# Weight sums on GpSimd, low parts in three-operand form, and seven-product down projections in four rounds instead of two

## The chip, the core and the metric

The kernel runs on one core of a Trainium2 chip. The metric is the device time of one execution in microseconds. Five engines work side by side and wait for each other through semaphores: TensorE (PE: matmuls into PSUM; PEld: its weight loads), VectorE (DVE), ScalarE (ACT), GpSimd (POOL) and SyncE (SP), which here issues most of the transfers from memory.

## The reference

Two layers of a hybrid decoder trunk on 528 tokens (16 learned meta tokens and 512 inputs) of width 1024, in float32. After the second layer only the 512 real tokens are kept. Each layer is an attention stage (a forgetting-attention group and a retention group of heads, one input and one output projection) and a feed-forward stage (FFN) of width 2816:

```python
def hybrid_layer(h, attn_norm_g, w_in, b_fgate, ret_gn_g, w_out,
                 ffn_norm_g, w_gate, w_up, w_down, cos, sin):
    ...
    mix = jnp.concatenate([fox_out, ret_out], axis=-1)
    h = h + jnp.einsum('blc,cd->bld', mix, w_out)

    hn = rmsnorm(h, ffn_norm_g)
    ff = jax.nn.silu(jnp.einsum('bld,df->blf', hn, w_gate)) * jnp.einsum('bld,df->blf', hn, w_up)
    return h + jnp.einsum('blf,fd->bld', ff, w_down)
```

The change touches the FFN alone. The final RMSNorm after layer 1 is untouched.

## The kernel before

**Layout.** Activations lie transposed: a tile `h[k]` holds 128 of the 1024 features as partitions and the tokens as columns. The 2816 columns of the FFN are 22 tiles of 128, numbered by `f`, 0 to 21.

**Three matmuls for one.** A float32 matmul is made as three matmuls in the format fp32r. Each operand is split into a high part (its rounding to fp32r, a copy on ScalarE) and a low part (the remainder, `src - hi`, a subtraction on VectorE); the products high x high, high x low and low x high are added in PSUM. The helper `split` (L154) does this for activations, `splits` (L940) for weights; the lines that appear in the profile are L155 for the former, L941 (rounding) and L942 (low part) for the latter. In the attention stage `convert` (L177) splits weights, and there the low parts of many weight tiles are made on GpSimd, in pieces of 128 columns (L208).

**Units.** From `f = 2` on (`PLAIN`), gate tile `f` and up tile `f` are computed together by the class `Unit` (L1055). The two output tiles, the two halves of the tokens (264 columns each, in layer 1 256) and the two halves of the 1024 input features form a 2 x 2 x 2 block product, and this is done with seven block products instead of eight. The price is sums of blocks ahead and behind. On the weight side they are, with `a` the gate weights and `b` the up weights in eight blocks of 128 x 128, `HB` = 4 of them a half:

```python
                    nc.vector.tensor_add(s[:, HB:NK], b[:, 0:HB], b[:, HB:NK])
                    nc.vector.tensor_sub(s[:, 0:HB], s[:, HB:NK], a[:, 0:HB])
                    splits(hi, lo, s)
```

(L1084 to L1086 in `make2`), and one more sum in `make3` (L1092) and in `make4` (L1098). So a unit has four sums of 128 x 512 on VectorE and splits of 1024, 1024, 1024 and 512 columns. On the token side the sums are made once a layer by `x_forms` (L905). Behind the products, `keep` (L1112) and `done` (L1127) add the partial results out of PSUM (L1124, L1131), apply the norm, SiLU and the product of gate and up (L1133 to L1139), and split the activation (L1143 to L1148). A layer has 20 units.

**Down projection in rounds.** The FFN width is worked off in `ROUNDS` of two or four tiles `f`. When the activations of a round are ready, their part of the down projection is computed during the units of the next round, one pair of output tiles of `h` beside each unit (four pairs, eight tiles). In a plain round `down` (L1181) makes 48 half-width matmuls for a pair and two additions to `h` (L1202 or L1204). In a round that stands in `SEVENTHS` the class `Pair` (L992) makes the pair in seven block products with 42 half-width matmuls. It needs sums of the down weights (L1012, L1013, L1018, L1020, 256 columns each), splits of 512, 512, 512 and 256 columns (L1011 to L1021), six additions to `h` (L1039, L1041), and sums of the two token halves of the activations, called forms 1 to 4, which `token_forms` (L963) makes when a unit of that round is done (L971, L982, and their splits). Form 1 is made in the first two units of a round, forms 2, 3 and 4 in the last two. Forms 2 and 3 are kept in the second token halves of `st["x"]`, which are no longer read then, form 4 in the tiles `sqh` and `sql`. Rounds 2 and 4 are in `SEVENTHS`; their pairs run beside the units of rounds 3 and 5. The last round is worked off at the end, by itself.

**What sets the order.** Only TensorE's order is written out by hand: the list `steps` in `ffn` (L861) is run in program order. The other engines' instructions are placed by a scheduler according to their dependencies and priorities, and each engine then works its queue in order. Weight tiles are jobs: `need(j)` (L935) converts job `j` and as many of the following as its `reach` says. High and low parts of weights go into two rings of buffers, three deep (`fwhi`, `fwlo`) and two deep (`whi`, `wlo`); a rounding waits until TensorE has read the buffer that it overwrites. Raw gate and down weights share four buffers (`raw`), up weights have two (`fraw`), the sums `S` two.

Of the kernel before, what the change touches and what calls it, by code (L numbers as in the profile page):

```python
# [10 lines left out]
F32 = mybir.dt.float32  # L11
F32R = mybir.dt.float32r
AF = mybir.ActivationFunctionType
ALU = mybir.AluOpType
# [11 lines left out]
NF = DFF // 128  # L26
ROUNDS = ((0, 2), (2, 6), (6, 10), (10, 14), (14, 18), (18, 22))
PLAIN = 2
SEVENTHS = (2, 4)
SEVEN = (0, 1, 2, 3)  # L30
HB = NK // 2
EPS = 1e-6
# [9 lines left out]
def hybrid_kernel(ctx, tc, x_t, w_in, w_fl, w_out, w_gate, w_up, w_down, vecs, b_fg, rope, decay, mask, ident, out_t):  # L42
# [92 lines left out]
    def sv(t, real, p0=0, p1=128):  # L135
        if real:
            return t[p0:p1, META:T]
        return t[p0:p1, 0:T].rearrange("p (a b) -> p a b", a=2)
# [15 lines left out]
    def split(hi, lo, src, pinned=False):  # L154
        return [pin(f, pinned).ins for f in (nc.scalar.copy(hi, src), nc.vector.tensor_sub(lo, src, hi.bitcast(F32)))]  # L155
# [705 lines left out]
    def ffn(l, st, real, last):  # L861
# [29 lines left out]
        def u_done(f):  # L891
            def go(ps):
                u = tt("tq")
                with tc.high_priority() if f == PLAIN - 1 else ExitStack():
                    nc.vector.scalar_tensor_tensor(sv(u, real), pv(ps, real), RSC, sv(st["R"], real), ALU.mult, ALU.mult)
                nc.vector.tensor_mul(sv(u, real), sv(u, real), sv(sgs[f], real))
                fh, fl = act_tile(f)
                split(sv(fh, real), sv(fl, real), sv(u, real))
                acts[f] = (fh, fl)
            return go  # L900

# [3 lines left out]
        def x_forms(k):  # L905
            def go():
                if k == 0:
                    st["t"] = [[fft(f"t{p}{i}", shape=(128, 2, 4, w)) for p in "hl"] for i in range(2)]
                s = fft("S", F32, (128, 6, w), 2)
                a, b = ((h[k][:, c0:c1], h[HB + k][:, c0:c1]) for c0, c1 in HC)  # L910
                g0, g1 = vcol(V_FFN + l * NK + k), vcol(V_FFN + l * NK + HB + k)
                with tc.issue_after(st["scaled"].ins) if real else ExitStack():
                    nc.scalar.activation(s[:, 0:2], two(h[k]), AF.Copy, scale=g0)
                nc.vector.tensor_sub(s[:, 2], s[:, 1], s[:, 0])
                for i in range(2):
                    nc.vector.scalar_tensor_tensor(s[:, 3 + i], b[1], g1, s[:, 1 + i], ALU.mult, ALU.subtract)
                nc.vector.scalar_tensor_tensor(s[:, 5], a[1], g1, s[:, 4], ALU.mult, ALU.subtract)
                th, tl = (t[:, k % 2] for t in st["t"][k // 2])
                split(th, tl, s[:, 2:6])
            return go  # L920

        def t_form(i):
# [16 lines left out]

        def splits(hi, lo, src):  # L940
            nc.scalar.copy(hi, src)  # L941
            nc.vector.tensor_sub(lo, src, hi.bitcast(F32))  # L942

        def product(j, o, x, bank, fresh, final, n=HB, done=None):

# [17 lines left out]
        def token_forms(f, u2):  # L963

            r = seventh(f)[0]
            f0 = ROUNDS[r][0]
            k = (f - f0) % 2
            first = [two(t)[:, 1] for t in acts[f0 + k]]
            if f - f0 < 2:
                halves[k] = u2  # L970
                nc.vector.tensor_sub(u2[:, 0], u2[:, 1], u2[:, 0])  # L971
                split(*first, u2[:, 0])
                forms[r, 1, k] = first
                return
            if k == 0:
                forms[r] = [tt("sqh", F32R), tt("sql", F32R)]
            (a, b), (c, d) = ([t[:, i] for i in range(2)] for t in (halves.pop(k), u2))
            four = [two(t)[:, k] for t in forms[r]]
            second, third = ([two(t)[:, 1] for t in st["x"][i]] for i in (2 + k, k))
            for n, o, x, y, (hi, lo) in ((3, b, d, b, third), (2, d, d, a, second), (4, c, c, d, four)):  # L980
                with tc.high_priority() if k and n < 4 else ExitStack():
                    nc.vector.tensor_sub(o, x, y)  # L982
                    split(hi, lo, o)
                forms[r, n, k] = hi, lo

        def form(r, n):
            return lambda k: forms[r, n, k]
# [67 lines left out]
        class Unit:  # L1055
# [24 lines left out]
            def make2(self, hi, lo):  # L1080
                a, b = self.t["a"], self.t["b"]
                s = self.t["s"] = fft("S", F32, (128, NK, 128), 2)
                with tc.high_priority() if self.f == PLAIN else ExitStack():
                    nc.vector.tensor_add(s[:, HB:NK], b[:, 0:HB], b[:, HB:NK])  # L1084
                    nc.vector.tensor_sub(s[:, 0:HB], s[:, HB:NK], a[:, 0:HB])
                    splits(hi, lo, s)  # L1086


            def make3(self, hi, lo):
                a, b = self.t["a"], self.t["b"]  # L1090
                with tc.high_priority(60) if self.f == PLAIN else ExitStack():
                    nc.vector.tensor_sub(b[:, 0:HB], a[:, 0:HB], b[:, 0:HB])  # L1092
                    splits(hi, lo, b)


            def make4(self, hi, lo):
                a, s = self.t["a"], self.t["s"]
                nc.vector.tensor_sub(a[:, HB:NK], a[:, HB:NK], s[:, 0:HB])  # L1098
                splits(hi, lo, a[:, HB:NK])

            def bank(self, n):
# [25 lines left out]
            def done(self):  # L1127
                e = self.t["e"]
                sg = tt("sg")
                with tc.high_priority():  # L1130
                    nc.vector.tensor_add(two(sg), self.t["zy"][:, :, 0:w], e[:, 0:2])  # L1131
                c = slice(t0, T)
                nc.vector.scalar_tensor_tensor(sg[:, c], sg[:, c], RSC, st["R"][:, c], ALU.mult, ALU.mult)  # L1133
                silu(sg[:, c], None if self.f < NF - 1 else ROOTS if last else LOGS)
                u = tt("tq")
                nc.vector.scalar_tensor_tensor(u[:, c], sg[:, c], RSC, st["R"][:, c], ALU.mult, ALU.mult)
                u2 = two(u)
                nc.vector.tensor_mul(u2[:, 0], self.t["x"][:, 0:w], u2[:, 0])
                nc.vector.tensor_mul(u2[:, 1], e[:, 2], u2[:, 1])  # L1139
                fh, fl = act_tile(self.f)  # L1140
                acts[self.f] = (fh, fl)
                if not seventh(self.f):
                    split(fh[:, c], fl[:, c], u[:, c])  # L1143
                    return
                if self.f - ROUNDS[seventh(self.f)[0]][0] < 2:
                    split(two(fh)[:, 0], two(fl)[:, 0], u2[:, 0])
                else:
                    split(fh[:, c], fl[:, c], u[:, c])  # L1148
                token_forms(self.f, u2)

            def head(self):
# [62 lines left out]
        for r, (f0, f1) in enumerate(ROUNDS):  # L1214
            for f in range(f0, f1):
                if f < PLAIN:
                    if f == 0:
                        st["first"] = range(len(jobs), len(jobs) + 3)
                    steps += dense_steps(w_gate[l, f], [(0, xs, NK, QC, g_done(f) if f else held.append)], banks=f == 1, own=own, far=f == 1, after=st["after"][2 * f])
                    steps += dense_steps(w_up[l, f], [(0, xs, NK, QC, u_done(f))], own=None if f else own, far=f == 0, after=st["after"][1 + 2 * f])  # L1220
                    continue
                for i in (f, f + 1) if f == PLAIN else (f,):
                    if i not in units:
                        units[i] = Unit(i)
                        steps += units[i].head()
                u = units[f]
                p, g0, g1 = fills.pop(0)
                seven = r - 1 in SEVENTHS and p in SEVEN
                after = r - 1 in SEVENTHS and p + 1 in SEVEN or r in SEVENTHS and f == f1 - 1 and 0 in SEVEN
                if seven:  # L1230
                    pair = Pair(r - 1, p)
                    u.rest()
                    pair.rest()
                    u.last()
                    jobs[u.w3]["reach"] = 5 if after else 4
                    d, m, t = pair.steps(), u.middle(), u.tail()
                    steps += d[0] + m[:NK] + d[2] + m[NK:] + d[1] + d[3] + t[:HB] + d[4] + t[HB:] + d[5] + d[6]
                    continue
                u.rest()
                steps += u.middle()  # L1240
                j = down_job(p, g0, g1)
                jobs[j]["reach"] = 4 if after else 3
                steps += down(j, 0, 2 * p, g0, g1, not real or f < PLAIN + 2)
                u.last()
                steps += u.tail()
                steps += down(j, 1, 2 * p + 1, g0, g1, f == PLAIN)
            fills = [(p, f0, f1) for p in range(NK // 2)]
# [379 lines left out]
```

## Time and profile before

| | |
|---|---|
| median of 3 runs | 1249.71 us (1249.49 to 1250.49) |
| span of the profiled execution | 1248.2 us, its granted TensorE clock 0.998 |
| TensorE, VectorE, ScalarE, GpSimd busy | 1236.6, 1062.2, 733.5, 294.6 us |
| FFN units of layer 0 | from about 320 to 609 us of the span |
| FFN units of layer 1 | from about 935 to 1213 us |
| GpSimd busy in these | 0 us |

The span runs from the first to the last instruction of the profiled execution; the runs that were timed lie 1.3 to 2.3 us above it. Busy times are sums of instruction spans without overlap. A line of a group gives the line of the kernel, the engine, the operation, the tile written and the tiles read, the shapes, the count, the total and the mean time, and the idle time of the engine before it. In a table of stages each line is a stretch of the span: its length, then busy time and instruction count of each engine, the granted clock and the share of the DMA engines. In a timeline the first number is the start in us, the second the time that the merged instructions cover.

### The profile page before, as it was taken

Reading aid. Unit: us, or ns where it says so; the run is one execution under the profiler, and the core shown is the slowest. Engines: PE = TensorE matmul, PEld = TensorE weight load, DVE = VectorE, ACT = ScalarE, POOL = GpSimd, SP = SyncE. Lnnn points to the kernel's source line nnn. Section 1 sums busy time; section 2 is a strip of 40 time slices with the busy share of each in tenths; the row PEclk is TensorE's granted clock in tenths of the full one; section 3 lists DMA queues with packets and bytes.
Section 4 is the critical chain, followed back from the end, with each engine's and each line's share of the span. In section 5 each row is a group of like instructions: output and inputs, shape, how many; then the busy total and the mean of one; then the engine's idle time right before and its main releaser. Section 6 shows DMA issues by size and latency. Waiting matters only on the chain.

```text
span 1248.2 us, 24164 instructions
## 1 busy us (share of the span) xinstructions
PE 1236.6 (99%) x9387; PEld 1192.1 (96%) x9387; DVE 1062.2 (85%) x2033; ACT 733.5 (59%) x1397; POOL 294.6 (24%) x568
## 2 busy tenths in 40 slices
PE   9999999999999999999999999999999999999997
PEld 9999999999999999999999989999799999999996
DVE  7887756889997999899876877568999989998996
ACT  7767655776544555455566766567765445454554
POOL 4555655440000000000035556554400000000000
PEclk9999999999999999999999999999999999999999
DMA  6222222222433233322312222231414333333322
GB/s 238 68 77 69 78 69 85 60 85 72 133 119 102 85 102 118 103 86 85 114 65 85 63 84 75 68 94 52 141 54 135 111 102 102 100 104 102 102 69 69
DMA packets 43347, 116.25 MB, mean 93 GB/s; under 512 B 5088, under 2 KB 9952, under 8 KB 43232
## 3 DMA queue, kind: packets, MB, share of 16 engines
q1 hardware_dynamic: 42800, 114.41, 28.8%
q8 instruction: 74, 1.21, 0.4%
q14 instruction: 41, 0.34, 0.1%
q10 hardware_dynamic: 432, 0.29, 0.1%
HBM read 112.58 MB, written 2.10 MB: 92 GB/s over the span
## 4 chain that ended last, share of the span: by engine, by line
PE 90%; DVE 5%; ACT 2%; DMA 1%; issue 1%; SPq 0%; ACTq 0%; DVEq 0%
PE psd L231 28%; PE psa L953 22%; PE psd L953 15%; PE psd L1197 8%; PE psa L231 5%; PE psa L1197 3%; PE psa L452 2%; PE psa L619 2%; PE psa L549 1%; PE psa L753 1%; PE psa L789 1%; DMA raw<-w_down 1%; DVE wlo L942 1%; DVE fwlo L942 0%; PE psa L312 0%
## 5 line engine op out<-in xcount | busy, mean ns | idle before, releaser
L208 POOL TENSOR_TENSOR wlo<-raw,whi 128x128 fp32r<-128x128 f32 x488 | 254.6, 557 | 212.2 <-ACT whi L204 212.2
L231 PE MATMUL psd<-xh,whi 128*128 128x264 f32 (+1 forms) x696 | 169.7, 313 | 0.0
L231 PE MATMUL psd<-xh,wlo 128*128 128x264 f32 (+1 forms) x696 | 161.0, 301 | 0.0
L231 PE MATMUL psd<-xl,whi 128*128 128x264 f32 (+1 forms) x696 | 160.6, 300 | 0.0
L231 PEld LDWEIGHTS psd<-xh,whi 128*128 128x128 f32 x696 | 112.6, 190 | 3.3 <-ACT whi L204 0.3
L231 PEld LDWEIGHTS psd<-xh,wlo 128*128 128x128 f32 x696 | 111.1, 188 | 4.4
L231 PEld LDWEIGHTS psd<-xl,whi 128*128 128x128 f32 x696 | 111.7, 189 | 2.5
L941 ACT CAST fwhi<-raw 128x512 fp32r<-128x512 f32 (+2 forms) x88 | 66.2, 757 | 72.3 <-PE psd L953 28.7
L204 ACT CAST whi<-raw 128x512 fp32r<-128x512 f32 (+1 forms) x140 | 82.1, 612 | 32.5 <-PE psd L231 17.3
L127 POOL MEMSET kc<- 64x528 f32 x4 | 2.1, 534 | 367.5 <-PE psd L1197 367.3
L942 DVE TENSOR_TENSOR fwlo<-raw,fwhi 128x512 fp32r<-128x512 f32 (+2 forms) x88 | 75.1, 854 | 7.5 <-ACT fwhi L941 7.4
L941 ACT CAST whi<-raw 128x1024 fp32r<-128x1024 f32 (+2 forms) x72 | 56.8, 789 | 37.6 <-PE psd L953 21.1
L1117 ACT COPY e<-psa 128x264 f32<-128x264 f32 (+1 forms) x120 | 44.9, 374 | 53.5 <-PE psa L953 51.9
L953 PE MATMUL psa<-th,fwhi 128*128 128x264 f32 (+1 forms) x248 | 70.4, 284 | 0.0
L953 PE MATMUL psa<-tl,fwhi 128*128 128x264 f32 (+1 forms) x248 | 70.1, 283 | 0.0
L953 PE MATMUL psa<-th,fwlo 128*128 128x264 f32 (+1 forms) x248 | 70.1, 283 | 0.0
L953 PE MATMUL psa<-th,whi 128*128 128x264 f32 (+1 forms) x232 | 65.4, 282 | 0.0
L942 DVE TENSOR_TENSOR wlo<-raw,whi 128x1024 fp32r<-128x1024 f32 (+1 forms) x72 | 64.1, 893 | 1.5 <-ACT whi L941 1.4
L953 PE MATMUL psa<-tl,whi 128*128 128x264 f32 (+1 forms) x232 | 65.4, 282 | 0.0
L953 PE MATMUL psa<-th,wlo 128*128 128x264 f32 (+1 forms) x232 | 65.3, 281 | 0.0
L566 ACT ACTIVATE pr<-pr,nmax 128x144 f32<-128x144 f32 (+1 forms) x64 | 36.8, 575 | 45.7 <-DVE nmax L553 26.3
L941 ACT CAST fwhi<-S 128x1024 fp32r<-128x1024 f32 (+1 forms) x34 | 28.8, 846 | 34.0 <-PE psa L953 14.3
(442 smaller groups left out, 4381.7 us busy)
## 6 DMA issues: line engine op xcount, KB each, us to landing
raw<-w_in SPq DMA_DIRECT2D x54, 512.0 KB, 3.5
raw<-w_gate SPq DMA_DIRECT2D x44, 512.0 KB, 3.5
fraw<-w_up SPq DMA_DIRECT2D x40, 512.0 KB, 3.5
raw<-w_down SPq DMA_DIRECT2D x80, 256.0 KB, 3.7
raw<-w_out SPq DMA_DIRECT2D x16, 512.0 KB, 3.5
h<-x_t SPq DMA_DIRECT2D x8, 264.0 KB, 4.5
dec<-decay SPq DMA_DIRECT2D x8, 264.0 KB, 2.7
raw<-w_up SPq DMA_DIRECT2D x4, 512.0 KB, 3.9
```

Of the source, the lines that this page charges most:

```text
L204: pin(nc.scalar.copy(hi, job["raw"][:, c0:c1]), pinned)
L208: pin(sub(lo[:, c:c + step], job["raw"][:, c0 + c:c0 + c + step], hi[:, c:c + step].bitcast(F32)), pinned)
L231: nc.tensor.matmul(ps[1][b][:, 0:c1 - c0], w[:, wk, :], x[:, c0:c1], start=(k == 0 and i == 0), stop=(k == n - 1 and i == 2))
L452: nc.tensor.transpose(ps[:, 128 * j:128 * j + 128], src[:, o:o + 128], idt)
L549: nc.tensor.matmul(sc[0:nq, 0:c1 - c0], qq[:, q0:q0 + nq], kk[:, c0:c1], start=(i == 0), stop=(i == 1))
L566: nc.scalar.activation(pr, pr, AF.Exp, bias=nmax[0:nq], scale=-1.0, accum_out=rsum)
L619: nc.tensor.matmul(po[:, c0:SEQ], v[:, j, :], pp[:, j, META + c0:T], start=(j == 0 and i == 0), stop=(j == 4))
L941: nc.scalar.copy(hi, src)
L942: nc.vector.tensor_sub(lo, src, hi.bitcast(F32))
L953: nc.tensor.matmul(bank()[:, 0:b.shape[-1]], a[:, o + k, :], b, start=(fresh and k == 0 and i == 0), stop=(k == n - 1 and i == 2), skip_gr ...
L1117: nc.scalar.copy(self.t["e"][:, i], self.t["x"][:, 0:w])
L1197: nc.tensor.matmul(v[:, 0:c1 - c0], a[:, s * n + k, :], b[:, c0:c1], start=(k == 0 and i == 0), stop=(k == n - 1 and i == 2))
```

## The change

It has four parts.

1. The four weight sums of a unit go to GpSimd, each as four instructions of 128 x 128 (`aside`).
2. In the FFN the low parts are made with `scalar_tensor_tensor`, `(src * 1.0) - hi`, in place of `tensor_sub`: in `splits` and in `halve`, which replaces `split` there. They stay on VectorE, the roundings on ScalarE.
3. `SEVENTHS` goes from two rounds a layer to four: rounds 1, 2, 3 and 4. The pairs of all rounds but the first (two tiles wide) and the last are then made in seven products.
4. Since a round in `SEVENTHS` can now follow another, the tiles of forms 2, 3 and 4 may still be read by the pairs of the round before. `later_form` makes one form; where the round before is in `SEVENTHS` too, the forms of the third unit and form 4 of both units are made during the last unit of the round, behind the products that last read their tiles. Form 4 is now computed as c - a from the tiles that are there, forms 2 and 3 as before.

```diff
-SEVENTHS = (2, 4)
+SEVENTHS = (1, 2, 3, 4)
...
         def splits(hi, lo, src):
             nc.scalar.copy(hi, src)
-            nc.vector.tensor_sub(lo, src, hi.bitcast(F32))
+            nc.vector.scalar_tensor_tensor(lo, src, 1.0, hi.bitcast(F32), ALU.mult, ALU.subtract)
+
+        def halve(hi, lo, src):
+            return [f.ins for f in (nc.scalar.copy(hi, src), nc.vector.scalar_tensor_tensor(lo, src, 1.0, hi.bitcast(F32), ALU.mult, ALU.subtract))]
+
+        def aside(op, out, p, q):
+            for k in range(out.shape[1]):
+                op(out[:, k], p[:, k], q[:, k])
...
             if f - f0 < 2:
                 halves[k] = u2
                 nc.vector.tensor_sub(u2[:, 0], u2[:, 1], u2[:, 0])
-                split(*first, u2[:, 0])
+                halve(*first, u2[:, 0])
                 forms[r, 1, k] = first
                 return
-            if k == 0:
+            halves[k] = halves[k], u2
+            if r - 1 not in SEVENTHS:
+                for n in (3, 2, 4):
+                    later_form(r, n, k)
+            elif k:
+                for n in (2, 3):
+                    later_form(r, n, k)
+
+        def later_form(r, n, k):
+            (a, b), (c, d) = ([t[:, i] for i in range(2)] for t in halves[k])
+            if n == 4 and k == 0:
                 forms[r] = [tt("sqh", F32R), tt("sql", F32R)]
...
+            o, x, y = {2: (a, d, a), 3: (b, d, b), 4: (c, c, a)}[n]
+            hi, lo = [two(t)[:, k] for t in forms[r]] if n == 4 else [two(t)[:, 1] for t in st["x"][k if n == 3 else 2 + k]]
+            with tc.high_priority() if k and n < 4 else ExitStack():
+                nc.vector.tensor_sub(o, x, y)
+                halve(hi, lo, o)
+            forms[r, n, k] = hi, lo
+
+        def later_forms(r, n, *ks):
+            return [lambda k=k: later_form(r, n, k) for k in ks] if r in SEVENTHS and r - 1 in SEVENTHS else []
...
-                    nc.vector.tensor_add(s[:, HB:NK], b[:, 0:HB], b[:, HB:NK])
-                    nc.vector.tensor_sub(s[:, 0:HB], s[:, HB:NK], a[:, 0:HB])
+                    aside(nc.gpsimd.tensor_add, s[:, HB:NK], b[:, 0:HB], b[:, HB:NK])
+                    aside(nc.gpsimd.tensor_sub, s[:, 0:HB], s[:, HB:NK], a[:, 0:HB])
                     splits(hi, lo, s)
...
-                    nc.vector.tensor_sub(b[:, 0:HB], a[:, 0:HB], b[:, 0:HB])
+                    aside(nc.gpsimd.tensor_sub, b[:, 0:HB], a[:, 0:HB], b[:, 0:HB])
...
-                nc.vector.tensor_sub(a[:, HB:NK], a[:, HB:NK], s[:, 0:HB])
+                aside(nc.gpsimd.tensor_sub, a[:, HB:NK], a[:, HB:NK], s[:, 0:HB])
...
-                    steps += d[0] + m[:NK] + d[2] + m[NK:] + d[1] + d[3] + t[:HB] + d[4] + t[HB:] + d[5] + d[6]
+                    i = r if f == f1 - 1 else None
+                    steps += (d[0] + m[:NK] + d[2] + m[NK:] + d[1] + later_forms(i, 2, 0) + d[3] + t[:HB] + d[4]
+                              + later_forms(i, 3, 0) + t[HB:] + d[5] + d[6] + later_forms(i, 4, 0, 1))
```

More of the change, by code (lines that the diff above doesn't have):

```diff
@@ L897, in go @@
                 fh, fl = act_tile(f)
-                split(sv(fh, real), sv(fl, real), sv(u, real))
+                halve(sv(fh, real), sv(fl, real), sv(u, real))
                 acts[f] = (fh, fl)
@@ L918, in go @@
                 th, tl = (t[:, k % 2] for t in st["t"][k // 2])
-                split(th, tl, s[:, 2:6])
+                halve(th, tl, s[:, 2:6])
             return go
@@ L971, in token_forms @@
                 nc.vector.tensor_sub(u2[:, 0], u2[:, 1], u2[:, 0])
-                split(*first, u2[:, 0])
+                halve(*first, u2[:, 0])
                 forms[r, 1, k] = first
                 return
-            if k == 0:
-                forms[r] = [tt("sqh", F32R), tt("sql", F32R)]
[L977 to L984, printed above, removed]
+            halves[k] = halves[k], u2
[8 more added lines that the diff above has]
+            if n == 4 and k == 0:
+                forms[r] = [tt("sqh", F32R), tt("sql", F32R)]
+            o, x, y = {2: (a, d, a), 3: (b, d, b), 4: (c, c, a)}[n]
[6 more added lines that the diff above has]
+            return [lambda k=k: later_form(r, n, k) for k in ks] if r in SEVENTHS and r - 1 in SEVENTHS else []
         def form(r, n):
@@ L1142, in done @@
                 if not seventh(self.f):
-                    split(fh[:, c], fl[:, c], u[:, c])
+                    halve(fh[:, c], fl[:, c], u[:, c])
                     return
                 if self.f - ROUNDS[seventh(self.f)[0]][0] < 2:
-                    split(two(fh)[:, 0], two(fl)[:, 0], u2[:, 0])
+                    halve(two(fh)[:, 0], two(fl)[:, 0], u2[:, 0])
                 else:
-                    split(fh[:, c], fl[:, c], u[:, c])
+                    halve(fh[:, c], fl[:, c], u[:, c])
                 token_forms(self.f, u2)
```

## The prediction

> **What bounds the kernel now.** I read the page first (engine shares, slices, chain), then the busy times of the engines by stage, the waits of TensorE in the FFN stages, the groups of VectorE by shape, and two stretches of the timeline in which GpSimd and VectorE work side by side.
>
> ```profile
> span 1248.2 us, 24164 instructions
> PE 1236.6 (99%) x9387; PEld 1192.1 (96%) x9387; DVE 1062.2 (85%) x2033; ACT 733.5 (59%) x1397; POOL 294.6 (24%) x568
> ...
> DVE  7887756889997999899876877568999989998996
> ...
> POOL 4555655440000000000035556554400000000000
> ...
> PE 90%; DVE 5%; ACT 2%; DMA 1%; issue 1%; SPq 0%; ACTq 0%; DVEq 0%
> ```
>
> TensorE is the bound: 99% busy, 90% of the chain. GpSimd works only in the two attention stretches; in both FFN stretches, which the change edits, it is idle. There VectorE's slices stand at 8 and 9, so the average of 85% hides a second engine near its limit. The stages show it:
>
> ```profile
> core 0: us, PE busy (x) PEld busy (x) DVE busy (x) ACT busy (x) POOL busy (x), PEclk, DMA share, GB/s
> ...
> 372.00:404.30 32.30, 32.30 (x267) 32.30 (x267) 25.85 (x43) 14.58 (x23) 0.00 (x0) 1.00 0.33 98
> 404.30:436.50 32.20, 32.20 (x267) 32.20 (x266) 32.14 (x61) 16.49 (x31) 0.00 (x0) 1.00 0.28 83
> 436.50:497.90 61.40, 61.40 (x506) 61.40 (x506) 61.03 (x107) 31.80 (x49) 0.00 (x0) 1.00 0.33 105
> ...
> 985.40:1016.30 30.90, 30.90 (x217) 28.86 (x216) 25.73 (x42) 14.36 (x23) 0.00 (x0) 1.00 0.37 116
> ...
> 1047.50:1106.80 59.30, 59.30 (x489) 58.51 (x489) 58.87 (x105) 30.38 (x49) 0.00 (x0) 1.00 0.34 107
> ...
> sum 566.50, PE 566.50 PEld 556.87 DVE 538.12 ACT 286.43 POOL 0.00; mean PE 40.46 PEld 39.78 DVE 38.44 ACT 20.46 POOL 0.00
> ```
>
> The sum is over all stages from the end of unit 2 to the end of unit 21 in both layers. A line is two units with plain down rounds (372 to 404.3, 985.4 on), two units that also make token forms (404.3 on), or four units with seven-product down rounds (436.5 on, 1047.5 on). In the last kind VectorE is busy 61.03 of 61.40 us: it only just keeps up, while ScalarE is at half and the clock is 1.00. TensorE still waits for nobody there:
>
> ```profile
> PE psd L1197 <- DVE al L155: 0.2, 1, 0.2
> PE psd L1197 <- ACT ah L155: 0.2, 1, 0.2
> ```
>
> These are all of TensorE's waits from 320 to 1213 us. So seven products pay in full today, but VectorE has 566.5 - 538.1 = 28 us left in both FFNs, nearly all in plain units.
>
> **What TensorE gains.** A plain pair of output tiles is 2 x 4 x 3 x 2 = 48 half-width matmuls, a seven-product pair 7 x 2 x 3 = 42. By the stages a plain unit lasts 32.30/2 = 16.15 us against 61.40/4 = 15.35, in layer 1 30.90/2 = 15.45 against 59.30/4 = 14.83: 0.6 to 0.8, I take 0.70. Rounds 1 and 3 (units 2 to 5 and 10 to 13, whose pairs run in the next round) become seven-product ones: 8 pairs a layer, 16 in all, 11.2 us. If TensorE stays the bound, the FFN stages take 555.3 us and the kernel, counted from the median of 1249.7 (the profiled span is 1.5 us below it), 1238.5.
>
> **What VectorE loses and gains.** Its groups:
>
> ```profile
> L1092 DVE TENSOR_TENSOR fraw<-raw,fraw 128x512 f32<-128x512 f32 x40 | 27.3, 684 | 0.0
> L1085 DVE TENSOR_TENSOR S<-S,raw 128x512 f32<-128x512 f32 x40 | 27.3, 684 | 0.2 <-DMA raw<-w_gate 0.2
> L1098 DVE TENSOR_TENSOR raw<-raw,S 128x512 f32<-128x512 f32 x40 | 27.3, 683 | 0.0
> L1084 DVE TENSOR_TENSOR S<-fraw 128x512 f32<-128x512 f32 x40 | 27.0, 684 | 0.3 <-DMA fraw<-w_up 0.3
> L942 DVE TENSOR_TENSOR wlo<-raw,whi 128x1024 fp32r<-128x1024 f32 x32 | 39.0, 1219 | 1.5 <-ACT whi L941 1.4
> L942 DVE TENSOR_TENSOR fwlo<-raw,fwhi 128x512 fp32r<-128x512 f32 x48 | 32.8, 683 | 0.0
> L1012 DVE TENSOR_TENSOR S<-raw 128x256 f32<-128x256 f32 x16 | 6.7, 419 | 3.1 <-DMA raw<-w_down 3.1
> L1041 DVE TENSOR_TENSOR h<-psa,h 128x264 f32<-128x264 f32 x32 | 13.6, 426 | 0.1
> L1204 DVE TENSOR_TENSOR h<-psd,h 128x528 f32<-128x528 f32 x19 | 13.3, 702 | 0.9 <-PE psd L1197 0.8
> L982 DVE TENSOR_TENSOR tq<-tq 128x264 f32<-128x264 f32 x12 | 5.1, 424 | 0.0
> L1133 DVE SCALAR_TENSOR_TENSOR sg<-sg,R 128x528 f32<-128x528 f32 x20 | 14.0, 700 | 0.0
> L155 DVE TENSOR_TENSOR al<-tq,ah 128x528 fp32r<-128x528 f32 x18 | 12.6, 702 | 0.8 <-ACT ah L155 0.7
> ```
>
> In a queue an instruction costs the distance of starts, not its duration. The stretch that also prices the sharing with GpSimd gives it:
>
> ```profile
> 879.65 0.83 DVE L825 SCALAR_TENSOR_TENSOR d<-d,gn,r 128x512 f32<-128x512 f32 x1
> ...
> 879.88 3.17 POOL L208 TENSOR_TENSOR rql<-raw,rqh 128x128 fp32r<-128x128 f32 x4
> ...
> 880.58 0.77 DVE L818 TENSOR_TENSOR d<-d,sg 128x512 f32<-128x512 f32 x1
> ...
> 882.03 0.69 DVE L155 TENSOR_TENSOR mxl<-d,mxh 128x512 fp32r<-128x512 f32 x1 [0.69 <-ACT mxh L155]
> ...
> 882.64 1.83 DVE L208 TENSOR_TENSOR wlo<-raw,whi 128x512 fp32r<-128x512 f32 x2
> ...
> 883.01 3.53 POOL L208 TENSOR_TENSOR rkl<-raw,rkh 128x128 fp32r<-128x128 f32 x4
> ...
> 884.39 1.82 DVE L208 TENSOR_TENSOR fwlo<-raw,fwhi 128x512 fp32r<-128x512 f32 x2
> ...
> 886.13 0.68 DVE L843 TENSOR_TENSOR h<-psd,h 128x512 f32<-128x512 f32 x1
> ```
>
> The one at 882.03 lasts 0.69 and the next starts 0.61 later: 0.08 of each duration overlaps. So 512 columns cost 0.604, 1024 cost 1.14, 528 cost 0.62, 256 and 264 cost 0.34 and 0.345.
>
> - Sums of gate and up weights leave: 4 x 40 x 0.604 = 96.6 us off.
> - A seven-product pair adds four sums of 256 columns (L1012 and its like), three low parts of 512 and one of 256, five additions of a half (L1041) and a full one: 3 x 0.604 + 5 x 0.338 + 5 x 0.346 + 0.62 = 5.85. It saves one low part of 1024 and two full additions, 1.14 + 1.24 = 2.38. 16 x 3.47 = 55.5 us on.
> - Token forms in two more rounds a layer: in the first two units three instructions of 264 replace one of 528 (+0.41 each), in the other two come six (2.07 each): 4.97 a round, four rounds, 19.9 us on.
> - Low parts in three-operand form: L1133 (three operands, both tensors in SBUF) takes 700 ns for 528 columns, L155 702. Free.
>
> VectorE's own work becomes 538.1 - 96.6 + 55.5 + 19.9 = 516.9 us, below TensorE's 555.3. ScalarE gets more roundings, but it is busy 286 of 566 us. Later forms are made behind the products that last read their tiles and are due a unit later; I cost the order at nothing.
>
> The Trainium skill ("Vector Engine (DVE) Microarchitecture Reference", "Points that are easy to get wrong") says that the three-operand form with two SBUF sources wider than bf16 runs at half throughput. The rows L1133 and L155 contradict it.
>
> **What GpSimd's pieces cost VectorE.** GpSimd gets 16 pieces a unit, 640 in all. What one costs alone, and what both engines do together:
>
> ```profile
> L208 POOL TENSOR_TENSOR wlo<-raw,whi 128x128 fp32r<-128x128 f32 x488 | 254.6, 557 | 212.2 <-ACT whi L204 212.2
> ```
>
> Its own time is no bound: 16 x 0.557 = 8.9 us of a 15 us unit. But from 882.64 to 886.13 four queued VectorE instructions of 512 columns take 3.49 us, 0.87 each and not 0.604, and GpSimd's pieces take 0.88 each: the two engines take turns, and every piece lets VectorE stand 0.27 us. From 879.65 on the delays are (0.83 - 0.69) + (0.77 - 0.69) + 0 + 4 x 0.27 = 1.30 us for eight pieces, 0.16 each. The line with the tile d, gn, r is a three-operand one and waits as well. The bounds of the price are thus 0 (the piece falls beside an instruction that reads PSUM, or beside an idle VectorE) and 0.27.
>
> The Trainium skill ("SBUF — State Buffer", "Who interferes with whom") says that a VectorE instruction with two SBUF inputs and a GpSimd instruction that reads SBUF share a port pair, and that the second to come is blocked for the whole of the first. The trace agrees in kind; in size a piece of 557 ns costs 0.27, not 0.557, and by 0.557 on every piece 640 of them would cost 356 us.
>
> Two prices decide. VectorE has 555.3 - 516.9 = 38.4 us to give, 0.060 us a piece; above that it is the bound. At (566.5 - 516.9)/640 = 0.078 the whole gain is eaten. With a seven-product down pair in its unit VectorE runs nine instructions from PSUM (six additions to h, L1124, L1131, L1138), beside which a waiting piece goes free; with two long ones, some ten of 16. The other six meet a queue without a hole and cost 0.27: 1.62 us a unit, 0.101 a piece, 64.8 us. That is 516.9 + 64.8 = 581.7 against 566.5: +15.2, so **1265 us**. I take this value because it lies between the bounds and because in the units that count VectorE has almost no idle time into which pieces could fall: the six units from 404.3 to 497.9 hold 32.14 + 61.03 = 93.2 us of its work; without their sums (6 x 2.42) and forms (2 x 2.07), and with a seven-product pair in two more of them (2 x 3.47), that is 81.5, or 13.6 a unit, and with the new forms (4.97/4) 14.8 of 15.35 us. From 0.085 to 0.13 a piece the time is 1254 to 1283.
>
> The chain gets longer too: eight pieces before the first mixed rounding, up to 8 x 0.88 = 7 us where VectorE took 1.2. The cover is that roundings wait for weight buffers that TensorE frees, not for sums:
>
> ```profile
> ACT fwhi L941 <- PE psa L953: 40.2, 15, 3.9
> ```
>
> Without that cover each unit would lie up to 5.8 - 3.9 = 2 us later; this is in the upper end of the range.
>
> **Rivals.** *TensorE stays the bound (faster).* The pieces fall into holes, or queued three-operand instructions keep the port pair. For it speaks one stretch:
>
> ```profile
> 26.68 0.84 DVE L428 SCALAR_TENSOR_TENSOR z<-z,R 8x528 f32<-8x528 f32 x1
> 27.45 0.69 DVE L465 SCALAR_TENSOR_TENSOR tq<-tq,R 128x528 f32<-128x528 f32 x1
> 28.07 0.69 DVE L479 SCALAR_TENSOR_TENSOR tq<-tq,R 128x528 f32<-128x528 f32 x1
> ...
> 26.03 3.66 POOL L208 TENSOR_TENSOR wlo<-raw,whi 128x128 fp32r<-128x128 f32 x3
> ```
>
> Behind L428 two three-operand instructions follow at 0.69, undelayed, while three pieces take 3.66 us. The change makes all low parts such instructions. Against it: sums and differences of pairs and forms stay two-operand, and GpSimd needs its 16 turns somewhere. Under 0.060 a piece the time is 1238.5; chance 0.36. Between 0.074 and 0.081 it comes out level, 0.09.
>
> *Every piece pays as in the stretch at 880 us.* 0.16 x 640 = 102.4: 619.3 against 566.5, 1302 us. Against it: that stretch has no PSUM instruction until its end. From 1283 up, 0.11.
>
> *Three-operand low parts take two steps a column.* From 512 to 1024 columns L942 grows by 536 ns; a unit has 3584 + 528 columns of low parts, so 8 x 0.536 = 4.3 us a unit, 172 us over 40, above 1400. L1133 speaks against it: 0.01. This is what the rule of the Trainium skill on that form would do here.
>
> **How the numbers follow.** My forecast has 0.43; slower by more than 0.2% (2.5 us, about what this measurement can tell) is 0.43 + 0.11 + 0.01 = 0.55, level 0.09, faster 0.36. The forecast's own range is 1254 to 1283; to hold the time eight times in ten it reaches down to the first rival, 1237, and up to 1290.
>
> **What would show it.** In the units of rounds 2 to 4 VectorE busy all the time and units longer than 15.35 us; low parts above 1220 and 684 ns; TensorE waiting for weight low parts; GpSimd pieces near 0.9 us. I am wrong if these units still last 15.3 and 14.8 us with VectorE showing idle time: then pieces cost less than 0.060 us.

## The result and the profile after

The changed kernel takes 1324.55 us (median of 4 runs, 1323.62 to 1325.96) against 1249.82 (median of 4): a ratio of 1.0599, 95% interval 1.0583 to 1.0614, slower by 75 us. The direction was forecast, the size was not: 1265 was said, and 1290 as the upper end. All times below are medians of four runs, but for the kernel with the sums left out, where one of the four took 6870.92 us and the median is that of the other three.

The page of the changed kernel, the lines that answer to those of before:

```profile
span 1321.7 us, 25373 instructions
PE 1259.3 (95%) x9483; PEld 1208.6 (91%) x9483; DVE 1120.3 (85%) x2105; ACT 757.6 (57%) x1477; POOL 727.1 (55%) x1208
...
DVE  7877747896999999999867776478969999999996
...
POOL 4555655507757474757055556555195666657540
...
PE 48%; DVE 41%; issue 5%; ACT 3%; POOL 2%; DMA 1%; DVEq 0%; SPq 0%; ACTq 0%; POOLq 0%
```

VectorE's average is the same 85%, and it says nothing: the chain tells that VectorE now holds 41% of the time and TensorE 48%, not 5% and 90%. GpSimd works through both FFNs.

The stages of layer 0 that answer to the first three lines of before's table. The end of a unit is here the start of its addition L1131 (now L1149), and a stretch has the name of the units behind whose ends it lies: units 6 and 7 run from the end of unit 6 to the end of unit 8. So the lines are units 6 and 7, 8 and 9, and 10 to 13:

```profile
core 0: us, PE busy (x) PEld busy (x) DVE busy (x) ACT busy (x) POOL busy (x), PEclk, DMA share, GB/s
389.30:420.90 31.60, 31.60 (x262) 31.60 (x261) 31.53 (x55) 16.56 (x30) 22.74 (x32) 1.00 0.32 101
420.90:456.50 35.60, 32.38 (x245) 31.34 (x244) 34.04 (x61) 17.39 (x31) 20.76 (x32) 0.95 0.26 90
456.50:525.70 69.20, 64.80 (x506) 63.27 (x506) 67.69 (x118) 34.30 (x61) 43.00 (x64) 0.98 0.30 92
```

Units 10 to 13 do nearly the same matmuls as before (506 records both times) and last 69.2 us, not 61.4. Now the FFN stages as a whole, from the end of unit 2 to the end of unit 21 in both layers; first the kernel before, then the changed one:

```profile
sum 566.20, PE 566.20 PEld 556.57 DVE 537.73 ACT 286.43 POOL 0.00; mean PE 283.10 PEld 278.29 DVE 268.86 ACT 143.22 POOL 0.00
```

```profile
330.10:641.40 311.30, 294.37 (x2318) 288.39 (x2317) 301.94 (x510) 155.95 (x269) 190.31 (x277) 0.98 0.30 93
980.50:1288.00 307.50, 288.58 (x2291) 279.98 (x2291) 299.37 (x507) 154.66 (x269) 190.13 (x275) 0.98 0.29 93
sum 618.80, PE 582.95 PEld 568.37 DVE 601.31 ACT 310.61 POOL 380.44; mean PE 291.48 PEld 284.18 DVE 300.66 ACT 155.31 POOL 190.22
```

The stages are 52.6 us longer. The rest of the 73.5 us between the spans lies ahead of them: unit 2 ends at 330.1 and not at 320.4, and from the end of unit 21 to the end of unit 2 in layer 1 it is 980.5 - 641.4 = 339.1 us, not 935.4 - 608.9 = 326.5. These are 9.7 and 12.6 us at the two starts of the FFN, and 1.4 are won back at the very end.

The groups of VectorE and GpSimd show what a row looks like when two engines get in each other's way (mean ns of one):

```profile
L942 DVE SCALAR_TENSOR_TENSOR fwlo<-raw,fwhi 128x512 fp32r<-128x512 f32 x72 | 58.4, 812 | 3.0 <-ACT fwhi L941 2.9
...
L1154 DVE SCALAR_TENSOR_TENSOR tq<-sg,R 128x528 f32<-128x528 f32 x20 | 18.6, 929 | 0.0
...
L1149 DVE TENSOR_TENSOR sg<-psd,e 128x528 f32<-128x528 f32 x20 | 14.0, 698 | 0.0
```

```profile
L949 POOL TENSOR_TENSOR S<-S,raw 128x128 f32<-128x128 f32 x160 | 128.6, 833 | 2.9 <-DMA raw<-w_gate 2.9
L949 POOL TENSOR_TENSOR S<-fraw 128x128 f32<-128x128 f32 x160 | 104.4, 683 | 191.2 <-DVE tl L945 71.6 <-issue 38.8 <-DVE fwlo L942 37.3
```

A low part of 512 columns took 683 ns before and takes 812; L1154 (L1136 before) took 703 and takes 929. L1149, as wide but with one input in PSUM, takes 698, no more than before. The pieces of GpSimd suffer too: 683 and 833 ns.

TensorE's waits in the FFNs (who, for whom: us in total, times, longest) were 0.4 us before. Now they are 49 us, and the three largest groups are:

```profile
PE psa L960 <- ACT e L1135: 15.3, 13, 6.3
PE psd L960 <- DVE al L945: 13.6, 8, 1.9
PE psa L960 <- DVE h L1059: 9.9, 16, 2.0
```

### The profile page after: what moved, and what is told of

Same layout as the page of the kernel before. It is cut to its first block, busy times and chain, and to the rows that moved or that the text cites. A ratio compares the mean times of both kernels' runs of the same rounds, so it can differ in the third digit from the quotient of the medians.

```text
span 1321.7 us, 25373 instructions
## 1 busy us (share of the span) xinstructions
PE 1259.3 (95%) x9483; PEld 1208.6 (91%) x9483; DVE 1120.3 (85%) x2105; ACT 757.6 (57%) x1477; POOL 727.1 (55%) x1208
## 4 chain that ended last, share of the span: by engine, by line
PE 48%; DVE 41%; issue 5%; ACT 3%; POOL 2%; DMA 1%; DVEq 0%; SPq 0%; ACTq 0%; POOLq 0%
PE psd L231 22%; PE psa L960 8%; DVE fwlo L942 8%; DVE wlo L942 6%; PE psd L960 4%; PE psa L231 3%; DVE h L1059 3%; DVE tq L1154 2%; DVE al L945 2%; PE psa L452 2%; DVE sg L1151 2%; POOL S L949 2%; PE psa L619 2%; PE psd L1215 2%; DVE sg L1149 1%
## 5 line engine op out<-in xcount | busy, mean ns | idle before, releaser
L208 POOL TENSOR_TENSOR wlo<-raw,whi 128x128 fp32r<-128x128 f32 x488 | 254.7, 557 | 212.4 <-ACT whi L204 195.5
L949 POOL TENSOR_TENSOR S<-fraw 128x128 f32<-128x128 f32 x160 | 104.4, 683 | 191.2 <-DVE tl L945 71.6
L949 POOL TENSOR_TENSOR raw<-raw,S 128x128 f32<-128x128 f32 x160 | 102.0, 668 | 84.1 <-issue 66.2
L949 POOL TENSOR_TENSOR S<-S,raw 128x128 f32<-128x128 f32 x160 | 128.6, 833 | 2.9 <-DMA raw<-w_gate 2.9
L941 ACT CAST fwhi<-raw 128x512 fp32r<-128x512 f32 (+2 forms) x112 | 74.7, 681 | 62.5 <-PE psd L960 38.3
L942 DVE SCALAR_TENSOR_TENSOR fwlo<-raw,fwhi 128x512 fp32r<-128x512 f32 (+2 forms) x112 | 98.5, 879 | 4.3 <-ACT fwhi L941 4.2
L949 POOL TENSOR_TENSOR fraw<-raw,fraw 128x128 f32<-128x128 f32 x160 | 101.1, 661 | 0.0
L945 ACT CAST ah<-tq 128x264 fp32r<-128x264 f32 (+3 forms) x60 | 30.7, 511 | 92.1 <-DVE tq L1157 45.7
L942 DVE SCALAR_TENSOR_TENSOR wlo<-raw,whi 128x1024 fp32r<-128x1024 f32 (+1 forms) x80 | 73.2, 915 | 2.3 <-ACT whi L941 2.2
L941 ACT CAST whi<-raw 128x1024 fp32r<-128x1024 f32 (+1 forms) x80 | 55.1, 705 | 34.8 <-PE psd L960 16.0
L960 PE MATMUL psa<-th,whi 128*128 128x264 f32 (+1 forms) x232 | 68.9, 297 | 3.7 <-ACT e L1135 2.4
```

The source lines that it names most:

```text
L208: pin(sub(lo[:, c:c + step], job["raw"][:, c0 + c:c0 + c + step], hi[:, c:c + step].bitcast(F32)), pinned)
L942: nc.vector.scalar_tensor_tensor(lo, src, 1.0, hi.bitcast(F32), ALU.mult, ALU.subtract)
L945: return [f.ins for f in (nc.scalar.copy(hi, src), nc.vector.scalar_tensor_tensor(lo, src, 1.0, hi.bitcast(F32), ALU.mult, ALU.subtract))]
L949: op(out[:, k], p[:, k], q[:, k])
L960: nc.tensor.matmul(bank()[:, 0:b.shape[-1]], a[:, o + k, :], b, start=(fresh and k == 0 and i == 0), stop=(k == n - 1 and i == 2), skip_gr ...
```

## The experiments

The theory after this comparison (A): each GpSimd piece that reads SBUF makes VectorE stand, VectorE becomes the bound of the units, and the pieces of the first units form a serial chain at the start of each FFN. The rivals: the order of the later forms alone makes TensorE wait (B); the form of the low parts decides who gets the port pair; any work of GpSimd disturbs, whether it reads or not; a turn costs the same whatever its width. Nine kernels were run.

**The sums left out.** Edit, from the changed kernel:

```diff
...
-                    aside(nc.gpsimd.tensor_add, s[:, HB:NK], b[:, 0:HB], b[:, HB:NK])
-                    aside(nc.gpsimd.tensor_sub, s[:, 0:HB], s[:, HB:NK], a[:, 0:HB])
-                    splits(hi, lo, s)
+                    splits(hi, lo, b)
...
-                    aside(nc.gpsimd.tensor_sub, b[:, 0:HB], a[:, 0:HB], b[:, 0:HB])
...
-                aside(nc.gpsimd.tensor_sub, a[:, HB:NK], a[:, HB:NK], s[:, 0:HB])
```

> The changed kernel without the four weight sums of a unit: they are left out and the splits take the weights as they come, so the gate and up outputs are not those of the reference; all else stays, the roundings, low parts, forms, four seven-product rounds. Theory A (VectorE is the bound, because each of the 640 GpSimd pieces makes it stand about 0.14 us in the units, and because the pieces form a serial chain at the start of each FFN): VectorE's own work is 516.9 us in the unit stages, so TensorE binds again, 1238 to 1243 us. Theory B (the later forms, made behind the products that last read their tiles, make TensorE wait whatever GpSimd does): units at the ends of rounds stay at 18 us, 1255 us or more.

Measured: 1242.26 us (median of three runs), ratio 0.9938 (0.9921 to 0.9954). Four seven-product rounds with their forms do run at TensorE's pace when nobody makes the sums; theory B falls.

**The pieces kept, but writing only.** Edit:

```diff
             for k in range(out.shape[1]):
-                op(out[:, k], p[:, k], q[:, k])
+                nc.gpsimd.memset(out[:, k], 0.0)
```

> The changed kernel with each of the 640 pieces replaced by a fill with zeros of the same 128 columns: the sums are left out, GpSimd writes as many columns and reads none. Theory A (the sharing is of reads): VectorE is not delayed, low parts of 512 columns stay at 0.68 us, 1243 to 1250 us, a little above the kernel without sums at 1242.7. Rival (any GpSimd instruction takes its turn): 1290 us or more.

Measured: 1239.02 us, ratio 0.9913 (0.9898 to 0.9928). GpSimd's pieces, VectorE's low parts, and the stages in this kernel:

```profile
L949 POOL MEMSET S<- 128x128 f32 x320 | 49.5, 206 | 115.4 <-DVE fwlo L942 51.2 <-DVE wlo L942 46.3 <-ACT fwhi L941 15.8
```

```profile
L942 DVE SCALAR_TENSOR_TENSOR fwlo<-raw,fwhi 128x512 fp32r<-128x512 f32 x72 | 49.5, 688 | 5.7 <-ACT fwhi L941 3.6
```

```profile
320.20:603.10 282.90, 282.90 (x2319) 282.48 (x2318) 267.80 (x508) 157.84 (x269) 41.70 (x264) 1.00 0.32 103
929.80:1202.70 272.90, 272.88 (x2288) 271.35 (x2287) 262.73 (x506) 156.87 (x269) 41.60 (x265) 1.00 0.31 104
sum 555.80, PE 555.77 PEld 553.82 DVE 530.52 ACT 314.71 POOL 83.31; mean PE 277.89 PEld 276.91 DVE 265.26 ACT 157.35 POOL 41.65
```

640 pieces of GpSimd that write as much as the sums cost nothing: low parts are back at 688 ns, TensorE is busy throughout, unit 2 ends at 320.2. The fills are also shorter than the sums (206 ns) and wait for no weights, so the run doesn't separate reading from length at the start of the FFN. In the units it does: 144 of VectorE's instructions with both inputs in SBUF run beside a fill, and none lasts over 12 ns more than is usual for its form. In the changed kernel 431 run beside a piece and 309 of them last over 60 ns more; of the VectorE instructions with an input in PSUM 245 run beside a piece, and none lasts over 10 ns more. So VectorE is delayed where both engines read SBUF and VectorE has both its inputs there. The Trainium skill ("SBUF — State Buffer", "Who interferes with whom") states just this limit, that a VectorE instruction with two SBUF inputs contends with a GpSimd instruction that reads SBUF and not with one that only writes; the trace agrees (688 ns against 812).

These stages also give the terms apart. VectorE executes nearly the same number of instructions in them as in the changed kernel (508 + 506 against 510 + 507) and is busy 530.5 us, not 601.3: 70.8 us are standing, 0.128 for each of the 552 pieces that lie in the stages.

**The sums back on VectorE, four rounds kept.** Edit: `aside` calls `nc.vector` on 512 columns.

> The changed kernel with the weight sums back on VectorE, 512 columns each; four rounds and three-operand form stay. Theory A: VectorE's own work is 516.9 + 96.6 = 613.5 us in the unit stages against 566.5 of TensorE before, so about 1250 + 47 = 1297 us, no wait of TensorE at the start of the FFN, and 27 us faster than the changed kernel. If GpSimd's relief were worth its price this would be slower than 1324.

Measured: 1312.33 us, ratio 1.0501 (1.0485 to 1.0517); the stages take 625.2 us with VectorE busy 610.8. In the direction of theory A, with 15 us more than expected: VectorE stands idle for 14.4 us in the stages though nothing runs on GpSimd there, and the expectation had no idle time. Four rounds are too much for VectorE with its sums, and moving all of them does not help: at 12 us less this kernel is faster than the changed one.

**The first two units' sums back on VectorE.** Edit: `aside` uses GpSimd where `self.f >= PLAIN + 2`, VectorE with 512 columns otherwise.

> The changed kernel with the sums of units 2 and 3 alone on VectorE, the other 18 units' on GpSimd. If the chain of pieces at the start of the FFN costs what the traces differ there (9.7 us in layer 0, 12.6 in layer 1), about 1302 us; if that time only moves into the units behind it, 1318 us or more.

Measured: 1305.27 us, ratio 1.0453 (1.0427 to 1.0479): 19.3 us less than the changed kernel. Unit 2 ends at 320.6 us as before, and the stages stay at 622.5 us. In the changed kernel the start looks like this (pieces of the chain in order of time: start, us, what), with TensorE's waits from 300 to 332 us behind it:

```profile
302.97 1.18 DVE tl L945
...
304.82 1.55 POOL S L949 x4
306.38 0.31 issue
306.69 2.31 POOL S L949 x3
...
309.38 2.27 POOL fraw L949 x3
311.66 2.65 POOL raw L949 x4
314.31 3.15 POOL S L949 x5
317.46 0.78 issue
318.23 1.27 POOL S L949 x3
...
322.13 0.38 ACT e L1135
```

```profile
PE psa L960 <- ACT e L1135: 7.7, 2, 6.3
```

The first sum waits for a buffer `S` that the token sums of `x_forms` hold until 304.2 us (their last low part, tl, L945). Then the pieces of units 2 and 3 come one behind another past 321 us, and roundings and TensorE wait for them. Here nothing lies ahead that could cover them.

**Two rounds, sums on GpSimd.** Edit, from the changed kernel: `SEVENTHS = (2, 4)`.

> The changed kernel with two seven-product rounds as before, so that only the sums are moved and the form of the low parts is changed. Theory A: VectorE has 538.1 - 96.6 + 640 x 0.14 = 531 us in the unit stages, under 566, so units last as before (16.1 and 15.4 us in layer 0); only the chain of pieces at the start of each FFN remains, 10 us a layer: 1270 us. Theory B (forms): 1250 us.

Measured: 1282.06 us, ratio 1.0257 (1.024 to 1.0274), 12 us more than expected. Of the 32 us above before, 9.4 and 12.6 are the two starts, the rest lies in units that were at VectorE's limit. Units 6 and 7, then 8 and 9 of layer 0:

```profile
382.20:414.00 31.80, 31.80 (x263) 31.80 (x263) 24.25 (x38) 14.25 (x23) 14.76 (x21) 1.00 0.32 100
414.00:447.90 33.90, 33.00 (x270) 32.69 (x269) 33.29 (x55) 17.12 (x31) 21.89 (x32) 1.00 0.25 79
```

Where VectorE has room (24.3 of 31.8 us) the pieces cost no time; in the units that also make forms it is full and they last 33.9 us, not 32.2. The expectation had added up VectorE's work over all units, 531 us of 566, and so spread its idle time over units that have none.

**Two rounds, the first two units' sums on VectorE.** Both edits together.

> Two seven-product rounds as before, low parts three-operand, sums of units 2 and 3 on VectorE, those of the other 18 units of a layer on GpSimd. Without the chain at the start, 19 us less than with all sums on GpSimd (as the same step gave with four rounds): 1263 us. What is left above 1250 is then the price of the pieces in the units that also make forms (8, 9, 16, 17), which lasted 16.7 and 17.1 us there against 16.1.

Measured: 1267.65 us, ratio 1.0144 (1.0127 to 1.0161), 4.6 us above the expectation. Unit 2 ends at 320.5 us, but units 2 and 3 of layer 1 last 12.7 and 16.1 us, not 9.8 and 13.5: part of the chain only moves to the next units. No version with sums on GpSimd comes down to the kernel before.

**Low parts with two operands.** Edit: `tensor_sub(lo, src, hi)` in `splits` and `halve`.

> The changed kernel with the low parts of the FFN as two-operand subtractions again. Theory A (both forms take turns with GpSimd alike, 0.26 us for each piece that meets one): 1322 to 1327 us, as the changed kernel. Rival (queued three-operand instructions keep the port pair, as one stretch of the profile before suggested): each of some 200 delayed low parts pays more often, 1335 us or more.

Measured: 1326.1 us, ratio 1.0608 (1.0592 to 1.0624), as the changed kernel. Its low parts of 512 columns:

```profile
L942 DVE TENSOR_TENSOR fwlo<-raw,fwhi 128x512 fp32r<-128x512 f32 x72 | 58.2, 809 | 3.2 <-ACT fwhi L941 3.1
```

809 against 812 ns: the form of the instruction is of no account. Undelayed three-operand instructions beside a piece, as in the stretch at 27 us that the prediction gave for the opposite, are no sign of a kept port: in the changed kernel too, 122 of the 431 instructions beside a piece are not delayed.

**Wider and narrower pieces.** Edits: one instruction of 512 columns for a sum; two instructions of 64 for a block.

> The changed kernel with each weight sum as one GpSimd instruction of 512 columns, 160 in all, not 640 of 128. Theory A: GpSimd holds VectorE off for as long as it streams, some 0.26 us for 128 columns and about 1.05 for 512, so a quarter of the turns at four times the price: 1310 to 1340 us, with delayed VectorE instructions of 512 columns near 1.7 us. Rival: the turn costs the same whatever its width, 160 x 0.26 = 42 us instead of 77: below 1295 us.

> The changed kernel with each sum in pieces of 64 columns, eight for one sum, 1280 in all. Theory A (GpSimd holds VectorE off for as long as it streams, and each VectorE instruction with two SBUF inputs can be met by one piece): about 0.13 us for each that is met, and up to twice as many met; VectorE's loss in the units between 50 and 77 us, so 1298 to 1325 us. Rival (a turn costs the same whatever its width, 0.26 us): more turns, 1340 us or more.

Measured: 1339.24 us, ratio 1.072 (1.0702 to 1.0738), with 512 columns, and 1333.42 us, ratio 1.067 (1.0652 to 1.0688), with 64. Two rows of the kernel with wide sums, then GpSimd's row of it and one of the kernel with narrow pieces:

```profile
L942 DVE SCALAR_TENSOR_TENSOR fwlo<-fraw,fwhi 128x1024 fp32r<-128x1024 f32 x22 | 41.8, 1899 | 0.7 <-ACT fwhi L941 0.5
...
L1153 DVE SCALAR_TENSOR_TENSOR tq<-sg,R 128x528 f32<-128x528 f32 x20 | 26.7, 1337 | 0.0
```

```profile
L948 POOL TENSOR_TENSOR fraw<-raw,fraw 128x512 f32<-128x512 f32 x40 | 75.0, 1876 | 0.0
```

```profile
L950 POOL TENSOR_TENSOR S<-S,raw 128x64 f32<-128x64 f32 x320 | 161.3, 537 | 0.9 <-DMA raw<-w_gate 0.9
```

For the three widths I counted in the traces the VectorE instructions of the stages with both inputs in SBUF (694 in each kernel) that last over 60 ns more than the same form does undisturbed, and by how much:

| columns of a piece | pieces in the stages | VectorE instructions delayed | mean delay | sum |
|---|---|---|---|---|
| 64 | 1112 | 533 | 0.12 us | 65 us |
| 128 | 550 | 307 | 0.25 us | 76 us |
| 512 | 136 | 108 | 0.89 us | 96 us |

The delay follows the width, 1.7 to 1.9 ns a column, so the rival of a fixed turn falls. Narrow pieces delay half as long and meet 1.7 times as many instructions: the sum moves little. What they save they lose in GpSimd's own time: the start of layer 0 is at 333.5 us instead of 330.1, and from unit 21 to the next unit 2 it is 989.0 - 643.8 = 345.2 instead of 339.1. My expectation of 1298 to 1325 had left that out.

## Why the prediction was right or wrong, step by step

**TensorE's gain: right.** 555.3 us were worked out for the stages of four seven-product rounds; with the pieces that only write they take 555.8, and the kernel takes 1239.02 where 1238.5 was given for the case that TensorE stays the bound. The rival with a chance of 0.36 has the right price; its condition, that pieces fall into holes or that queued instructions keep the port pair, is what failed. The two-operand run shows that the form of the low parts makes no difference, so the stretch at 27 us carried nothing.

**VectorE's own work: 13.6 us too low.** 516.9 was said, 530.5 is measured. The step that failed is "sums of gate and up weights leave: 96.6 us off": it took the sums of 40 units off a busy time whose stages begin at the end of unit 2, when the sums of the first units have already run. The stages of the kernel before hold 144 of the 160 sums, 87 us at 0.604 each, which is 9.6 of the 13.6. The other 4 us are not taken apart.

**The price of the pieces: a little low.** "Some ten of 16 go free, the other six cost 0.27" gives 64.8 us. The cost of a meeting was right (0.25 us), the count was not: 550 pieces delay 307 instructions, nine for 16 pieces. VectorE stands 70.8 us by the busy times. An instruction that reads PSUM does let a piece through free (L1149 above), but pieces come in bursts of eight and four and don't wait for such a moment. The 557 ns that the prediction took for a piece alone is a mean over disturbed and undisturbed ones; the sum did not use it.

**No idle time on VectorE: wrong by 17.5 us.** The sum took VectorE's time for the time of the stages. It stands idle for 618.8 - 601.3 us in them. In unit 9 of layer 0 (438.2 to 456.5 us, 18.3 us long) VectorE's waits and then TensorE's are:

```profile
DVE h L1059 <- PE psa L960: 1.2, 1, 1.2
DVE h L1059 <- PE psd L960: 0.3, 1, 0.3
```

```profile
PE psd L960 <- DVE al L945: 1.4, 1, 1.4
PE psd L960 <- ACT ah L945: 1.2, 1, 1.2
```

In this unit, at the end of a round, TensorE waits for the low part of the last activation, and when it goes on, VectorE waits for its results: two engines near their limit hand the wait back and forth. That is only part of the idle time. Over the stages of both layers VectorE waits 18.4 us (waits across an edge counted whole): 6.0 for TensorE's results, 10.3 for ScalarE, of which 7.8 for roundings of weights, and 2.1 for transfers. Why the roundings come late there is not shown. In the kernels whose VectorE is not behind (sums left out, pieces writing only) the same order of forms gives no units of 18 us, the longest last 16.1 and 15.7 us. I had costed that order at nothing, which is right only while VectorE keeps up.

**The path to TensorE: not the one named.** Long units, low parts above 684 ns and a busy VectorE came as the prediction said. TensorE's waits for weight low parts did not: they are 0.8 us, once. TensorE waits for the additions to `h`, for the activation's low part and for ScalarE's copy `e`.

**The chain of pieces: the step that failed most.** "The cover is that roundings wait for weight buffers that TensorE frees" fails at the start of the FFN, where 32 pieces run in a row with nothing ahead. The prediction said that up to 2 us a unit lay in the upper end of its range, but 40 units would make 80 us and the range ends 25 us above the forecast, so the chain was in fact put at almost nothing. The two starts cost 22.3 us, and the kernel is 19.3 us faster when units 2 and 3 are summed on VectorE.

Together: 1265 + 13.6 + 6.0 + 17.5 + 22.3 - 1.4 = 1323, and 1324.55 is measured.

**The comparison that was missing.** By the 0.128 us that VectorE stands for each piece, four pieces cost it 0.51 us, and the sum itself would cost it 0.604. Moving a sum off a full VectorE thus wins back 0.09 us of 0.60, a seventh. Measured against the run with all sums on VectorE it is a ninth: its busy time in the stages falls from 610.8 to 601.3 us, 9.5 us for 144 sums that cost 87. The two added seven-product rounds put 55.5 + 19.9 = 75.4 us on VectorE by the prediction's own terms, and it had 28 us left; such a relief cannot carry them. The prediction had both numbers and compared the price only with the time that TensorE leaves over, not with the work that is moved. The runs agree: four rounds with all sums on VectorE 1312.33, with all but the first two units' on GpSimd 1305.27. None of the versions that make the sums beats the kernel before.

What stays open: why the kernel with the sums left out is 3 us slower than the one with pieces that write (276.8 against 272.9 us in layer 1's stage), though it has less to do. The order of VectorE's queue differs between them; that was not tried by itself.

## What to carry to other kernels

Before work is moved from VectorE to GpSimd, set what VectorE loses for each piece against what it would have spent itself, for the instructions that it will be running then: with two SBUF inputs on both sides the relief here was a ninth to a seventh of the work moved. Add up an engine's load unit by unit and not over a stage, since idle time in one unit does not help a full one; and look at the start of a stage by itself, because there a slower engine's chain has nothing ahead to hide it. To see whether an engine disturbs by reading or by being busy, let it write the same tiles without reading: that one run set the engine's own work apart from its standing.

## What the runs showed of the hardware that had not been expected

The time for which GpSimd holds VectorE off is not the length of its instruction but 1.7 to 1.9 ns a column: 0.12, 0.25 and 0.89 us for pieces of 64, 128 and 512 columns. The Trainium skill ("SBUF — State Buffer", "Summary: rules for kernel authors") says that the one who comes second is blocked until the first has finished; here an undisturbed piece of 128 columns lasts 0.46 us (those of L208 beside no VectorE instruction with two SBUF inputs) and blocks for 0.25. Fills of 128 columns on GpSimd take 206 ns and delay no one. And TensorE's granted clock, 1.00 in all stages of before, is 0.95 in units 8 and 9 of the changed kernel, where it waits. In units 10 to 13 it is 0.98, and TensorE is busy 64.8 us for 506 matmul records, not 61.4. Whether the clock adds to the time was not tried by itself.
